# Moving the elementwise helpers of an expert layer from GpSimd to the vector engine, with dense weights split in two steps

## The chip, the cores and the metric

One core of one Trainium2 chip runs the whole kernel. The metric is device time in microseconds (us) of one execution, as the median of several runs. Beside the runs there is one profiled execution with its trace. TensorE is called PE, VectorE DVE, ScalarE ACT, GpSimd POOL, and SP is the engine that only issues transfers.

## The reference

The layer has 1024 latent tokens (and 256 context tokens) of width 1024. A front part (normalisation, an input projection, two groups of recurrent heads, an output projection) gives the stream `x1` and its normalised, modulated form `h2`. The change touches only the second half, an expert layer with 128 x 128 = 16384 experts, each one row `u` and one row `v` of 1024 numbers:

```python
q = (xb @ wq).reshape(PEER_BLOCK, PEER_HEADS, 2, PEER_QDIM // 2)
s = jnp.einsum('tphq,phkq->tphk', q, keys)          # 8 heads x 2 halves x 128 keys
top_s, top_i = lax.top_k(s, PEER_TOPK)              # 16 of each half
cand = top_s[:, :, 0, :, None] + top_s[:, :, 1, None, :]
best_s, best_c = lax.top_k(cand.reshape(...), PEER_TOPK)
idx = i1 * PEER_NKEYS + i2                          # 128 experts a token
g = jax.nn.softmax(best_s, axis=-1)
act = jax.nn.gelu(jnp.einsum('tpkd,td->tpk', u_tab[idx], xb), approximate=False)
return jnp.einsum('tpk,tpkd->td', g * act, v_tab[idx])
```

The result is added to the stream with a gate, and a last RMSNorm follows. All is in fp32.

## The kernel before

The eight blocks of 128 tokens are treated in two ways. **Three blocks (A) are gathered**: for each of the 3 x 128 expert slots, POOL fetches one row of `uv` (u and v side by side, 8 KB) for each of the 128 tokens by an indirect transfer (`fetch`, L996), DVE multiplies the u half with `h2` and sums (L1043), ACT makes gelu and gate (L1008, L1009), and DVE adds the gated v half to an accumulator (L1021). These 384 steps are one generator, `gather`; four row buffers (`uv`) circulate. **Five blocks (B, 640 tokens) are dense**: for all 128 chunks of 128 experts, PE computes U times h2 (L1077, tile `ua`), ACT takes gelu into `w` (L1118), a weight matrix of gates `gch` is multiplied in, and PE multiplies with V (L1465, tile `po`).

PE gets fp32 accuracy from three products of split operands: x = high + low, where ACT makes the high part by a copy (`uh`, `vh`, `wh`, `qhi`) and another engine subtracts it from x to make the low part (`ul`, `vl`, `wl`, `qlo`). One chunk of U needs 48 matmuls of 320 columns; its four quarters of 12 matmuls are what the generator `earlier` yields.

After the front part the stages are, in the order of the program:

- query stage of A (its query weights split with `qlo` on POOL, L1182), then the selection of A's experts (`select`), beside which the first chunks of U and the first gather steps run;
- query stage of B: 16 groups of query matmuls (`pq`), key scores (`sc`) and top-16 searches on DVE, with gather steps and U chunks between;
- selection of B, block by block, again with gather steps and U chunks between;
- building the gate matrices (`gtl`): 80 iterations, each four fp16 operations on DVE (L1354 to L1357: `o`, `oh`, `ol`, `oh`) over 8 tokens, and 16 small matmuls (`gb`) that read them one iteration later;
- a rest of U chunks with nothing else to do on PE; 84 of the 128 chunks (`early`) are computed ahead in all these stages and parked in DRAM (`d_A`);
- the dense stage: 16 groups of 8 chunks, each in two halves of V's columns. In the second half the weights of the next group are made (`produce`, `weights`, `weigh`), and the 44 chunks of U that are left are computed. At the end of each half five sums of `po` go into `accB` on DVE (L1472);
- the last group and the last norm.

Each engine runs its instructions in the order in which the program issues them, so the interleaving is the program's: there is no scheduler. It is steered by two planned clocks, `clock["PE"]` and `clock["DVE"]`. Each step adds its estimated time; `ticks` issues gather steps at given rates; `fill` issues quarters of U chunks as long as PE's clock is less than `lead` = 6 us ahead of DVE's, up to 320 quarters (`spare`).

In the version before, the low part of an early U chunk (`ul`, L1103) is made on POOL when the chunk before it runs, in two halves of 128x512; in B's query stage `qlo` is made on POOL; and while `share[0]` is 2 (B's query stage and selection) every second product of the gather is on POOL too (L1041), and ACT sums it (L1007). The accumulator of the gather lies in two of the eight PSUM banks (`accP`) until the dense stage begins.

## Time and profile before

| | us |
|---|---|
| median of 3 runs | 3157.88 |
| lowest, highest | 3156.48, 3166.47 |
| the profiled execution | 3155.61 |
| span of its trace | 3153.8 |

The trace has 46913 instructions; the mean granted TensorE clock is 0.957 of full speed. Busy times overlap between engines, so they do not add up to the span. A matmul's record covers its whole passage, and matmuls overlap; how fast PE works is read from the distance of their starts.

### The profile page before, as it was taken

How to read it: one execution, taken by the hardware profiler on the slowest of the kernel's cores; microseconds unless marked ns; L12 is line 12 of the kernel's file. 1: busy time of each engine (PE TensorE's matmuls, PEld its weight loads, DVE VectorE, ACT ScalarE, POOL GpSimd, SP SyncE). 2: the span in 40 equal slices, each digit the busy share in tenths (PEclk: the TensorE clock that was granted, in tenths of full speed). 3: DMA queues.
4: the chain of work that ended last, by engine and by line, in shares of the span. 5: the costliest groups of instructions: out<-in, count | busy, mean ns of one | idle time of the engine just before them, and what ended most of it. 6: DMA issues, size and time to landing. Idle time of an engine off the chain costs nothing.

```text
span 3153.8 us, 46913 instructions
## 1 busy us (share of the span) xinstructions
PE 2863.5 (91%) x16937; PEld 2522.2 (80%) x16937; DVE 2508.2 (80%) x4801; ACT 1330.0 (42%) x2915; POOL 997.2 (32%) x768
## 2 busy tenths in 40 slices
PE   7999799998997997878888889999999999999997
PEld 3799677777997987878888888888887788888875
DVE  6633344576798999999999958888888788888885
ACT  4622244564443454455555633333333333333332
POOL 1000113233456776644443432222222222222211
PEclk9999889999998998889999999999999999999998
DMA  6455487645367876768898899999999999999983
GB/s 234 127 187 169 142 258 229 218 144 191 107 245 260 289 275 222 248 234 311 320 318 299 334 367 342 350 339 339 342 344 339 319 331 336 336 338 340 339 301 104
DMA packets 391273, 856.56 MB, mean 272 GB/s; under 512 B 27512, under 2 KB 207352, under 8 KB 341632
## 3 DMA queue, kind: packets, MB, share of 16 engines
q1 hardware_dynamic: 309520, 372.91, 36.9%
q0 software_dynamic: 57600, 411.07, 35.0%
q10 hardware_dynamic: 23920, 69.59, 5.6%
q8 instruction: 133, 2.18, 0.3%
q14 instruction: 100, 0.82, 0.1%
HBM read 746.16 MB, written 107.30 MB: 271 GB/s over the span
## 4 chain that ended last, share of the span: by engine, by line
issue 23%; DVE 18%; PE 7%; POOL 7%; DMA 2%; ACT 1%; POOLq 0%; SPq 0%; DVEq 0%; ACTq 0%
POOL uv L996 7%; PE po L1465 5%; DVE ol L1356 4%; DVE uv L1043 3%; DVE accP L1021 2%; PE ua L1077 2%; DVE oh L1357 2%; DVE oh L1355 2%; DVE o L1354 2%; DMA vr<-uv 1%; DVE acc L1021 1%; DMA uv<-uv,idx 1%; DVE vl L1431 0%; DMA gch<-d_G 0%; ACT wh L1441 0%
## 5 line engine op out<-in xcount | busy, mean ns | idle before, releaser
L996 POOL DMA_INDIRECT uv<-uv,idx x384 | 456.8, 1190 | 1292.1 <-DVE acc L1021 883.6
L1465 PE MATMUL po<-vh,wh 128*128 128x512 f32 x1255 | 499.6, 398 | 50.5 <-DVE accB L1472 44.3
L1077 PE MATMUL ua<-hBhi,uh 128*128 128x320 f32 x2048 | 490.3, 321 | 36.0 <-ACT uh L1102 28.4
L1465 PE MATMUL po<-vl,wh 128*128 128x512 f32 x1255 | 497.8, 397 | 12.0 <-DVE vl L1431 11.9
L1077 PE MATMUL ua<-hBhi,ul 128*128 128x320 f32 x2048 | 479.7, 316 | 22.4 <-POOL ul L1103 22.2
L1465 PE MATMUL po<-vh,wl 128*128 128x512 f32 x1255 | 495.7, 395 | 0.0
L1043 DVE SCALAR_TENSOR_TENSOR uv<-uv,h2a 128x1024 f32<-128x1024 f32 x351 | 441.0, 1256 | 50.7 <-DMA uv<-uv,idx 50.4
L1077 PE MATMUL ua<-hBlo,uh 128*128 128x320 f32 x2048 | 477.9, 315 | 0.0
L1077 PEld LDWEIGHTS ua<-hBhi,uh 128*128 128x128 f32 x2048 | 354.1, 195 | 43.1 <-ACT uh L1102 31.0
L1077 PEld LDWEIGHTS ua<-hBhi,ul 128*128 128x128 f32 x2048 | 351.9, 193 | 27.2 <-POOL ul L1103 27.2
L1077 PEld LDWEIGHTS ua<-hBlo,uh 128*128 128x128 f32 x2048 | 354.7, 194 | 0.0
L1465 PEld LDWEIGHTS po<-vh,wh 128*128 128x128 f32 x1255 | 240.2, 191 | 109.5 <-DVE accB L1472 52.5
L1021 DVE SCALAR_TENSOR_TENSOR acc<-uv,act,acc 128x1024 f32<-128x1024 f32 x237 | 303.3, 1280 | 0.0
L1465 PEld LDWEIGHTS po<-vl,wh 128*128 128x128 f32 x1255 | 240.5, 192 | 64.3 <-DVE vl L1431 16.6
L1465 PEld LDWEIGHTS po<-vh,wl 128*128 128x128 f32 x1255 | 240.1, 191 | 50.9
L1103 POOL TENSOR_TENSOR ul<-ur,uh 128x512 fp32r<-128x512 f32 x170 | 239.3, 1431 | 76.5 <-ACT uh L1102 72.1
L1441 ACT ACTIVATE wh<-w 128x640 fp32r<-128x640 f32 x128 | 94.6, 739 | 396.6 <-DVE w L1438 358.1
L1430 ACT ACTIVATE vh<-vr 128x512 fp32r<-128x512 f32 x251 | 156.4, 625 | 147.7 <-PE po L1465 145.9
L1008 ACT ACTIVATE act<-act 128x1 f32<-128x1 f32 x384 | 75.9, 198 | 335.4 <-DVE uv L1043 333.6
L1021 DVE SCALAR_TENSOR_TENSOR accP<-uv,act,accP 128x1024 f32<-128x1024 f32 x144 | 184.5, 1281 | 13.4 <-ACT act L1009 13.4
L1338 ACT ACTIVATE gtl<-gb 128x512 f32<-128x512 f32 x160 | 160.6, 1113 | 70.1 <-PE gb L1336 58.0
L1442 DVE TENSOR_TENSOR wl<-w,wh 128x640 fp32r<-128x640 f32 x128 | 105.6, 825 | 105.3 <-ACT wh L1441 103.7
(387 smaller groups left out, 5547.1 us busy)
## 6 DMA issues: line engine op xcount, KB each, us to landing
ur<-uC SPq DMA_DIRECT2D x256, 256.0 KB
vr<-uv SPq DMA_DIRECT2D x256, 256.0 KB
d_G<-gtl ACTq DMA_DIRECT2D x80, 512.0 KB
gch<-d_G SPq DMA_DIRECT2D x64, 640.0 KB
d_A<-w ACTq DMA_DIRECT2D x84, 320.0 KB
w<-d_A SPq DMA_DIRECT2D x84, 320.0 KB
wm<-w_mod SPq DMA_DIRECT2D x32, 512.0 KB
qraw<-wq SPq DMA_DIRECT2D x32, 512.0 KB
```

The source lines that it names most:

```text
L996: G.indirect_dma_start(out=t.rearrange("p a d -> p (a d)"), out_offset=None, in_=A["uv"], in_offset=bass.IndirectOffsetOnAxis(ap=idxs[n][: ...
L1008: S.activation(acts[i], acts[i], AF.Gelu)
L1021: V.scalar_tensor_tensor(acc, v, act, acc, op0=ALU.mult, op1=ALU.add)
L1043: V.scalar_tensor_tensor(t, t, 1.0, h2s[n], op0=ALU.mult, op1=ALU.mult, accum_out=acts[i])
L1077: T.matmul(pt[:, :b - a], l[:, kt], m[:, kt, a:b], start=(kt == 0 and wi == 0), stop=(kt == KT - 1 and wi == 2))
L1103: usplit[0].tensor_tensor(ul[:, k], ur, uh[:, k].bitcast(F32), op=ALU.subtract)
L1338: S.activation(gt[:, :, tt:tt + 4].rearrange("p e t -> p t e"), pt.rearrange("p (t e) -> p t e", e=P), AF.Copy, scale=1.0 / 4096.0)
L1356: V.tensor_tensor(ol, oh, pairs(glT, b, t0), op=ALU.mult)
L1430: S.activation(vh, vr[n], AF.Copy)
L1441: S.activation(wh, w, AF.Copy)
L1442: V.tensor_tensor(wl, w, wh.bitcast(F32), op=ALU.subtract)
L1465: T.matmul(po, st[:, b * P:(b + 1) * P], m, start=(start and wi == 0), stop=(stop and wi == 2))
```

## The change

It has six parts. (1) The low part of an early U chunk is made by DVE, as one operation on 128x1024, just as the chunk's first matmuls are issued (`u_low` in `u_side`), and no longer by POOL a chunk ahead; U is loaded in pieces of 128x1024 in three buffers instead of 128x512 in six. (2) In B's query stage `qlo` is made by DVE; A's stays on POOL. (3) The share of the gather's products on POOL is gone: all are on DVE, and ACT's sum of them is gone. So POOL only fetches rows from the selection of A on. (4) The accumulator of the gather lies in SBUF, all eight PSUM banks serve the matmuls, and the copies out of PSUM (`settle`) are gone. (5) The planned DVE clock is charged 2.55 us for a gather step (before 2.35, and 1.75 while every second product was on POOL) and 0.3 us for each quarter of an early chunk. (6) Dense weights are made in two steps: `weights` is a generator that yields between the high part on ACT and the low part on DVE, and `weigh` is called at `b in (1, 3)` of each chunk and between the quarters of a dense U chunk.

```diff
             if i < total:
-                if share[0] and i % share[0] == 0:
-                    prods[i] = t
-                    G.tensor_tensor(t, t, h2s[n], op=ALU.mult)
-                else:
-                    V.scalar_tensor_tensor(t, t, 1.0, h2s[n], op0=ALU.mult, op1=ALU.mult, accum_out=acts[i])
+                V.scalar_tensor_tensor(t, t, 1.0, h2s[n], op0=ALU.mult, op1=ALU.mult, accum_out=acts[i])
...
-    ru = [eru.enter_context(tc.tile_pool(name="ru", bufs=6))]
+    ru = [eru.enter_context(tc.tile_pool(name="ru", bufs=3)), KT]
...
     def u_prep(c):
         if c >= P or isinstance(us[c], tuple):
             return
         uh = up.tile([P, KT, P], F32R, tag="uh", name="uh")
-        ul = up.tile([P, KT, P], F32R, tag="ul", name="ul")
-        for n, ur in enumerate(us[c]):
-            k = slice(4 * n, 4 * n + 4)
+        for k, ur in us[c]:
             S.activation(uh[:, k], ur, AF.Copy)
-            usplit[0].tensor_tensor(ul[:, k], ur, uh[:, k].bitcast(F32), op=ALU.subtract)
-        us[c] = (uh, ul)
+        us[c] = (uh, us[c])
+        if dense[0]:
+            u_low(c)
+
+    def u_low(c):
+
+        uh, parts = us[c]
+        if isinstance(parts, list):
+            ul = up.tile([P, KT, P], F32R, tag="ul", name="ul")
+            for k, ur in parts:
+                V.tensor_tensor(ul[:, k], ur, uh[:, k].bitcast(F32), op=ALU.subtract)
+            us[c] = (uh, ul)
 
     def u_side(c, ahead):
 
         cuts = cuts_of(nd)
+        u_low(c)
         pts = [ubank[0]("ua") for _ in cuts]
...
-            clock["DVE"] += 2.35 - (1.2 / share[0] if share[0] else 0)
+            clock["DVE"] += 2.55
...
             clock["PE"] += next(earlier)
+            clock["DVE"] += 0.3
...
-                    (G if g else V).tensor_tensor(lo, raw, hi.bitcast(F32), op=ALU.subtract)
+
+                    (G if g and ticking >= 0 else V).tensor_tensor(lo, raw, hi.bitcast(F32), op=ALU.subtract)
...
             wh = wp.tile([P, nd], F32R, tag="wh", name="wh")
+            S.activation(wh, w, AF.Copy)
+            yield
             wl = wp.tile([P, nd], F32R, tag="wl", name="wl")
-            S.activation(wh, w, AF.Copy)
             V.tensor_tensor(wl, w, wh.bitcast(F32), op=ALU.subtract)
             ws[c] = (wh, wl)
...
         def weigh():
-            while pend:
-                weights(pend.pop())
+
+            if pend and next(pend[0], True):
+                pend.pop(0)
...
             if c not in first:
                 for d in u_side(plan.index(c), True):
                     ticks(d, share_of)
-            pend.append(c)
+                    weigh()
+            while pend:
+                weigh()
+            pend.append(weights(c))
...
-                        if b == 1:
+                        if b in (1, 3):
                             weigh()
```

How many U chunks and gather steps stand in which stage of the program, counted from the two orders:

| stage | U chunks before | after | gather steps before | after |
|---|---|---|---|---|
| selection of A | 12.75 | 16.25 | 12 | 12 |
| query of B | 1.5 | 6.75 | 35 | 35 |
| selection of B | 23.25 | 33.75 | 31 | 31 |
| gate matrices | 41.5 | 23.25 | 62 | 62 |
| rest, with the first dense chunks | 8 | 7 | 9 | 7 |
| dense | 41 | 41 | 235 | 237 |

On POOL, around B's selection, the order before has, with `r` the index pattern that the selection starts with:

```order
L1041 TENSOR_TENSOR uv<-uv,h2a 128x1024
L1103 TENSOR_TENSOR ul<-ur,uh 128x512 x2
L832 IOTA r_10965 128x256
L996 DMA uv<-uv,idx_6695 128x2048
L1103 TENSOR_TENSOR ul<-ur,uh 128x512 x2
L996 DMA uv<-uv,idx_6695 128x2048
```

and the order after:

```order
L1175 TENSOR_TENSOR qlo<-qraw,qhi 128x1024 x15
L832 IOTA r_7697 128x256
L987 DMA uv<-uv,idx_6695 128x2048 x49
L832 IOTA r_11449 128x256
L987 DMA uv<-uv,idx_6695 128x2048 x31
```

The fetches stand behind no operation on tiles any more; the fifteen `qlo` left are A's.

On PE, in the middle of the gate matrices (about the 35th of the 80 iterations), the order before has a quarter or more of a U chunk after each iteration's products (`o` changes its number with the iteration):

```order
L1336 MATMUL gb<-o_15239,ol 128x128
L1077 MATMUL ua<-hBhi,uh 128x320 x2
L1077 MATMUL ua<-hBlo,uh 128x320 x2
L1077 MATMUL ua<-hBhi,ul 128x320 x2
L1077 MATMUL ua<-hBhi,uh 128x320 x2
```

and the order after goes from one iteration's products straight to the next one's:

```order
L1322 MATMUL gb<-o_16409,ol 128x128
L1321 LDWEIGHTS oh
L1321 MATMUL gb<-o_16490,oh 128x128
L1322 LDWEIGHTS ol
L1322 MATMUL gb<-o_16490,ol 128x128
```

From the 35th iteration to the 80th the order after has no U chunk: the 320 quarters have been issued before.

On DVE, at the end of a second half in the dense stage, the order before has the high and the low step of two weights and then the five sums:

```order
L1431 TENSOR_TENSOR vl<-vr,vh 128x512
L1438 TENSOR_TENSOR w<-w,gch 128x640
L1442 TENSOR_TENSOR wl<-w,wh 128x640
L1043 SCALAR_TENSOR_TENSOR uv,act<-uv,h2a 128x1024
L1021 SCALAR_TENSOR_TENSOR acc<-uv,act,acc 128x1024
L1431 TENSOR_TENSOR vl<-vr,vh 128x512
L1438 TENSOR_TENSOR w<-w,gch 128x640
L1442 TENSOR_TENSOR wl<-w,wh 128x640
L1472 TENSOR_TENSOR accB<-accB,po 128x512 x5
```

and the order after:

```order
L1412 TENSOR_TENSOR vl<-vr,vh 128x512
L1419 TENSOR_TENSOR w<-w,gch 128x640
L1027 SCALAR_TENSOR_TENSOR uv,act<-uv,h2a 128x1024
L1009 SCALAR_TENSOR_TENSOR acc<-uv,act,acc 128x1024
L1424 TENSOR_TENSOR wl<-w,wh 128x640
L1412 TENSOR_TENSOR vl<-vr,vh 128x512
L1419 TENSOR_TENSOR w<-w,gch 128x640
L1424 TENSOR_TENSOR wl<-w,wh 128x640
L1457 TENSOR_TENSOR accB<-accB,po 128x512 x5
```

The first of the two weights now has a gather step between its product and its low part; in the second the two still follow each other on DVE. Of the 128 weights, 29 have a gather step in between, and 99 have nothing.

## Rows read from the trace of the kernel before

**Rows 1.** Stretches: start:end length, busy PE, PEld, DVE, ACT, POOL; PEclk, DMA, GB/s.

```profile
861.00:977.00 116.00, 94.34 (x612) 93.15 (x612) 106.42 (x341) 51.22 (x91) 57.44 (x43) 0.91 0.66 235
977.00:1126.00 149.00, 142.62 (x977) 140.14 (x978) 140.91 (x622) 68.34 (x172) 108.55 (x64) 0.98 0.80 282
1126.00:1358.00 232.00, 182.22 (x1110) 175.84 (x1109) 228.90 (x615) 115.68 (x241) 152.83 (x99) 0.88 0.70 242
1358.00:1820.00 462.00, 401.27 (x3303) 386.93 (x3302) 453.92 (x518) 264.94 (x461) 193.21 (x148) 0.95 0.86 307
1820.00:1888.00 68.00, 61.26 (x395) 60.29 (x396) 34.77 (x45) 24.93 (x58) 27.21 (x20) 0.92 1.00 369
1888.00:3064.00 1176.00, 1124.77 (x5542) 970.11 (x5541) 1019.64 (x1409) 407.62 (x1006) 275.70 (x231) 0.98 0.95 337
3064.00:3154.00 90.00, 67.20 (x275) 52.47 (x274) 52.66 (x103) 22.15 (x52) 13.09 (x10) 0.90 0.33 114
```

**Rows 2.** Timeline of DVE and of POOL near 1405 us: start, length, instruction.

```profile
1405.42 2.50 POOL L1103 TENSOR_TENSOR ul<-ur,uh 128x512 fp32r<-128x512 f32 x2
...
1405.22 3.25 DVE L1356 TENSOR_TENSOR ol<-oh,glT 128x1024 f16<-128x1024 f16 x1
```

**Rows 3.** Groups by line, DVE, 1358 to 1820: count, busy us, mean ns, idle before.

```profile
L1356 DVE TENSOR_TENSOR ol<-oh,glT 128x1024 f16<-128x1024 f16 x80 | 124.5, 1556 | 2.8
...
L1355 DVE TENSOR_TENSOR oh<-io,i2T 128x1024 f16<-128x1024 f16 x80 | 64.5, 806 | 0.0
L1357 DVE TENSOR_TENSOR oh<-oh,ghT 128x1024 f16<-128x1024 f16 x80 | 62.4, 780 | 2.7
L1354 DVE TENSOR_TENSOR o<-io,i1T 128x1024 f16<-128x1024 f16 x80 | 59.1, 738 | 1.7 <-POOL io L1316 1.7
```

**Rows 4.** One line's instructions, L1356: shortest, median, longest in ns.

```profile
L1356 DVE TENSOR_TENSOR ol<-oh,glT x80: 691/692/3328, 1362.0 to 1818.6; 128x1024 f16<-128x1024 f16 x80
```

**Rows 5.** Groups by line and shape, DVE, 861 to 1358.

```profile
L899 DVE TENSOR_TENSOR oh<-oh 128x1024 bf16<-128x1024 bf16 x16 | 30.6, 1909 | 0.5
...
L895 DVE TENSOR_TENSOR oh<-r,rjb 128x2048 bf16<-128x2048 bf16 x8 | 18.3, 2285 | 0.0
...
L895 DVE TENSOR_TENSOR oh<-r,rib 128x2048 bf16<-128x2048 bf16 x8 | 9.7, 1218 | 0.0
```

**Rows 6.** Groups by line, 1888 to 3064: the gather's product on DVE.

```profile
L1043 DVE SCALAR_TENSOR_TENSOR uv<-uv,h2a 128x1024 f32<-128x1024 f32 x234 | 285.1, 1219 | 36.1 <-DMA uv<-uv,idx 35.8
```

**Rows 7.** Operations that move: groups on POOL, 861 to 1888; `qlo` on DVE, whole span.

```profile
L1103 POOL TENSOR_TENSOR ul<-ur,uh 128x512 fp32r<-128x512 f32 x170 | 239.3, 1431 | 76.5 <-ACT uh L1102 72.1 <-issue 3.5
...
L1041 POOL TENSOR_TENSOR uv<-uv,h2a 128x1024 f32<-128x1024 f32 x33 | 81.7, 2474 | 0.6
...
L1182 DVE TENSOR_TENSOR qlo<-qraw,qhi x2: 1215/1220/1226, 772.1 to 977.2; 128x1024 fp32r<-128x1024 f32 x2
```

**Rows 8.** PE's pace: two pieces of the chain; first and last `gb` of an iteration.

```profile
1821.21 27.81 PE ua L1077 x190
...
2363.00 37.03 PE po L1465 x162
...
1402.98 0.23 PE L1335 MATMUL gb<-o,oh 128*128 128x128 f16 x1
...
1403.85 0.22 PE L1336 MATMUL gb<-o,ol 128*128 128x128 f16 x1
```

**Rows 9.** Waits, 1888 or 1890 to 3064: waiter, ended by, us, times, longest.

```profile
DVE wl L1442 <- ACT wh L1441: 97.9, 119, 1.2
...
PE po L1465 <- DVE accB L1472: 42.7, 17, 5.3
```

**Rows 10.** Timeline at the end of a second half: DVE, then PE.

```profile
2435.66 0.83 DVE L1442 TENSOR_TENSOR wl<-w,wh 128x640 fp32r<-128x640 f32 x1 [0.80 <-ACT wh L1441]
2436.40 3.07 DVE L1472 TENSOR_TENSOR accB<-accB,po 128x512 f32<-128x512 f32 x5
...
2437.14 0.80 PE L1465 MATMUL po<-vh,wh 128*128 128x512 f32 x1 [5.31 <-DVE accB L1472]
```

More of the change, by code (lines that the diff above doesn't have):

```diff
@@ L927, in peer @@
     V, S, T, G, Y = nc.vector, nc.scalar, nc.tensor, nc.gpsimd, nc.sync
-    banks, ident, dr, rstd_of = [F["bank"]], F["ident"], F["dr"], F["rstd_of"]
-    bank = lambda name: banks[0](name)
+    bank, ident, dr, rstd_of = F["bank"], F["ident"], F["dr"], F["rstd_of"]
     d_h2, d_x1 = F["d_h2"], F["d_x1"]
@@ L933, in peer @@
     oA, oB = order[:ng], order[ng:]
-    es, esp = ExitStack(), ExitStack()
+    es = ExitStack()
     rows = {}
@@ L973, in peer @@
     gsA = [ga.tile([P, P], F32, name=f"g{n}") for n in range(ng)]
-    accs, psum = {}, []
+    accs = {}
     def row(name):
         return gr.tile([P, D], F32, tag="ha", name=name, bufs=3)
-    def settle(n):
-        t = row("acc")
-        for h in range(2):
-            S.activation(t[:, h * 512:h * 512 + 512], accs[n][:, h * 512:h * 512 + 512], AF.Copy)
-        accs[n] = t
     def gather_all():
         total = ng * P
-        uvs, h2s, acts, prods = {}, {}, {}, {}
+        uvs, h2s, acts = {}, {}, {}
         def fetch(i):
@@ L1014, in add @@
             if k == 0:
-                accs[n] = psum[0] if psum else row("acc")
+                accs[n] = row("acc")
             acc = accs[n]
@@ L1048, in gather_all @@
                 if i % P == 0:
-                    if psum:
-                        settle(i // P - 1)
                     fins.append(finish_steps(oA[i // P - 1], accs[i // P - 1], i == total))
@@ L1080, in project @@
                 yield 2 * 3 * sum(b - a for a, b in cuts) / 2400.0
-    us, wr, ubank, ulim, usplit = {}, {}, [bank], [early + 1], [G]
+    us, wr, ubank, ulim, dense = {}, {}, [bank], [early + 1], [False]
     first = [c for c in range(P) if (c + 1) * early // P != c * early // P]
@@ L1089, in u_load @@
             us[c] = []
-            for k in (0, 4):
-                ur = ru[0].tile([P, 4, P], F32, tag="ru", name="ur")
-                Y.dma_start(ur, A["uC"][plan[c]][:, k:k + 4])
-                us[c].append(ur)
+            m = ru[1]
+            for k in range(0, KT, m):
+                ur = ru[0].tile([P, m, P], F32, tag="ru", name="ur")
+                Y.dma_start(ur, A["uC"][plan[c]][:, k:k + m])
+                us[c].append((slice(k, k + m), ur))
     def u_prep(c):
@@ L1123, in early_all @@
             S.dma_start(d_A[n], wr.pop(c))
-    share = [0]
     gather, earlier = gather_all(), early_all()
@@ L1272, in afterA @@
         gr = es.enter_context(tc.tile_pool(name="gr", bufs=1, side="right"))
-        F["esp"].close()
-        pb = esp.enter_context(tc.tile_pool(name="pb", bufs=6, space=PSUM))
-        pc = esp.enter_context(tc.tile_pool(name="pc", bufs=1, space=PSUM))
-        banks[0] = lambda name: pb.tile([P, 512], F32, tag="b", name=name)
-        psum.append(pc.tile([P, D], F32, name="accP"))
         prime()
@@ L1374, in peer @@
     acc = hB2.tile([P, nb, D], F32, name="accB")
-    ru[0] = es.enter_context(tc.tile_pool(name="ru2", bufs=2))
+    ru[:] = es.enter_context(tc.tile_pool(name="ru2", bufs=2)), KT // 2
     ulim[0] = P
-    usplit[0] = V
-    for n in list(accs):
-        if accs[n] is psum[0]:
-            settle(n)
-    psum.clear()
-    esp.close()
+    dense[0] = True
+    F["esp"].close()
     pa = es.enter_context(tc.tile_pool(name="pa", bufs=8 - len(cuts_of(nd)), space=PSUM))
```

6 lines of the change are left out of this document (removed).

## The prediction

> **What bounds the kernel now.** I first cut the span into stretches and read the busy times of each [rows 1]. The change touches nothing before the selection of A at 861 us and nothing but one helper after 3064, so two parts count: the early stages from 861 to 1888 (1027 us) and the dense stage from 1888 to 3064 (1176 us).
>
> In the early stages DVE is the bound of three of the five stretches: it is busy 106 of 116 us in A's selection, 229 of 232 in B's selection and 454 of 462 in the gate matrices, while PE is busy 94, 182 and 401 [rows 1]. In B's query stage both are full (143 and 141 of 149), and in the rest PE alone works. The longer engine's busy times add to 106 + 143 + 229 + 454 + 61 = 993 us; the stretches take 1027, so 34 us (3.4%) are lost where the two wait for each other.
>
> The second thing to see is that DVE's busy time there is not all work. While POOL subtracts (`ul`, 2.50 us from 1405.42), an fp16 product on DVE that starts at 1405.22 takes 3.25 us and ends with it [rows 2]; the same line's median is 0.69 [rows 4]. The four fp16 lines hold 310.5 us in 320 instructions, which at 0.69 would be 221: 90 us too many [rows 3]. In the selections the 1024-wide sums take 30.6 us for 16, where 0.69 each gives 11, and one line takes 18.3 us with `rjb` and 9.7 with `rib`, the same shape eight times each: another 28 us [rows 5]. Comparing each DVE instruction with the shortest of its line and shape, I get 18, 4, 57 and 99 us in the first four stretches, 178 in all. B's query stage has nearly none, although POOL is busy 109 of its 149 us; its top-16 searches read one tensor.
>
> In the dense stage DVE is busy 1020 us, waits 98 us for ACT before the low part of a weight [rows 9] and 36 us for fetched rows [rows 6]: 1154 of 1176. So DVE's chain fills this stage, though PE is busy 1125. PE waits 42.7 us in 17 places for the sums of `po` [rows 9]; in one of them it stands for 5.31 us, while DVE waits 0.80 for ACT, makes `wl` and only then sums [rows 10].
>
> **Part by part: POOL is emptied.** If only operations on tiles hold DVE up, all 178 us go. That the fetches don't is seen in the dense stage: POOL fetches for 276 us there [rows 1], and the gather's product has a mean of 1219 ns [rows 6]. That row is of one kind of DVE operation; the fp16 ones are never seen beside fetches alone for long, so the gain lies between 178 us and what remains if a fetch holds DVE like a subtraction, which is a rival below. I take 178.
>
> The Trainium skill (GPSIMD Engine Reference, section Key points) says that GpSimd shares its SBUF interfaces with VectorE and contends with DVE instructions that have two SBUF inputs. The trace agrees for the subtractions (0.69 to 3.25 us); read as a rule for the fetches too, it would leave about 58 us, which the 1219 ns speak against.
>
> **What DVE gets instead.** 85 low parts of U, 15 `qlo` and 33 products, each some 1.2 us: `qlo` on DVE took 1.22, the product 1.22 [rows 7, 6], less a few hundredths since the next starts before an operation's end. That is 133 x 1.2 = 160 us. DVE's sum falls by 18 us, and 2 of the 149 early gather steps move to the dense stage (2 x 2.4 us).
>
> **Where the U chunks go.** A chunk is 48 matmuls at 27.81/190 = 0.146 us [rows 8], 7.0 us of PE. With the dearer planned DVE clock PE's chunks are issued earlier: 57 stand ahead of the gate matrices where 38 did, and the last 46 of the 80 iterations have none (the table and order above). So I add each stretch anew, PE beside DVE, and the longer one counts:
> - A's selection: PE 16.25 x 7.03 = 114; DVE 106 - 18 + 16 x 1.2 = 107. Longer: 114.
> - B's query: PE 143 - 1.5 x 7 + 6.75 x 7.03 = 180; DVE 141 - 4 + (15 + 18 + 7) x 1.2 = 185. Longer: 185.
> - B's selection: PE 33.75 x 7.03 = 237 and about 5 for 27 other matmuls; DVE 229 - 57 + (15 + 34) x 1.2 = 231. Longer: 242.
> - Gate matrices: one iteration without POOL's delays is (454 - 99)/80 = 4.44 us of DVE; an iteration's 16 small matmuls take about 0.93 us (0.87 from first to last start [rows 8]). The first 34: PE 23.25 x 7.03 + 34 x 0.93 = 195; DVE 34 x 4.44 + 23 x 1.2 = 179. The other 46: DVE 204, PE 43. Longer: 399.
> - Rest: 68 - 7 = 61.
>
> The sum is 114 + 185 + 242 + 399 + 61 = 1001 us, 8 more than the 993 of before: what DVE gains in the gate matrices (454 to 399) is lost again, since PE becomes the bound ahead of them and stands nearly empty in their second half. How much the engines lose to each other can't be read from the trace of before. It is bounded by the 34 us of now, if the lockstep is no worse; by 15, if emptying POOL and PSUM takes most of it away; and by 7% (75 us), since DVE now makes `ul` at the very place where PE needs it. I take 36, near the value seen: 1037, so +10 us (from -11 to +49).
>
> **Weights in two steps.** One wait for ACT costs 97.9/119 = 0.82 us [rows 9]. The idea would remove all of it, but the order shows that 99 of the 128 low parts still follow their product directly on DVE, so that DVE waits for ACT as before; 29 have a gather step in between. That saves 29 x 0.82 = 24 us of a chain that fills the stage; two more gather steps cost 5. I take -17 for the dense stage (1159), between 0, if the time comes back as waiting for fetched rows, and -43, if all of PE's waits for the sums go. PE's own pace is no obstacle: 3570 matmuls at 37.03/162 = 0.229 and 1972 at 0.146 make 1105 us [rows 8, 1].
>
> **Edits costed at nothing.** U in pieces of 512 KB instead of 256: the same bytes in the same buffer space, and the issue stands at the same place of the queue; it is hidden by the two chunks (14 us) between load and use. If that cover went, PE would wait for `uh`. The accumulator in SBUF: one DVE operation as before. ACT loses 33 sums and the copies out of PSUM; ACT is busy about half of the time [rows 1].
>
> The sum: 3155.6 + 10 - 17 = 3149 against the profiled execution; the median of the runs stands 2.3 us higher, which is inside the error, and I say **3150**.
>
> **Rivals.**
> 1. *The low part of U on the path (slower).* In the stages before the 35th iteration DVE has 702 us of work against PE's 736, and each of some 79 chunks can begin only when DVE, in its own order, has made `ul`. DVE's pieces are uneven: a step of the selection and one or two gather steps make 5 to 7 us in a row. For it: DVE was busy 97 to 99% there when it was the bound. Against it: the program issues PE's work 6 us ahead of DVE's, and `uh` is ready a chunk earlier. At 0.5 us a chunk beyond my 36 us it costs 40: 3190. It decides the sign from about 0.2 us a chunk (16 us: 3166).
> 2. *Both losses go (faster).* With POOL no longer in the chain and eight PSUM banks the early loss is 15 us, and the freed 24 us on DVE let it catch up before each second half ends, so that PE's waits vanish: 3155.6 - 11 - 43 = 3102. For it: 24 us over 15 such ends are 1.6 us each, against 42.7/15 = 2.8. Against it: DVE stays the fuller chain.
> 3. *Fetches hold DVE as well, so that emptying POOL does less than it says.* POOL was busy 539 us in the early stages [rows 1]; 147 fetches of 1.2 us are a third of that, so a third of 178, 58 us, would stay: 3207. The 1219 ns speak against it.
>
> **How the numbers follow.** My forecast has 0.42, with a range of its own of 3136 to 3164; rival 1 has 0.26, rival 2 has 0.24, rival 3 has 0.05, and 0.03 is left for a load that comes late. The range has to reach most of rivals 1 and 2: 3105 to 3190. A measurement of this kernel can tell about 0.3%, 9.5 us, from no change. Faster than 3148: 0.18 of the forecast's chance and nearly all of rival 2, 0.41. Within: 0.20 of the forecast's and 0.06 of the rivals' mild ends, 0.26. Slower: 0.33.
>
> **What would show it.** Right: the fp16 lines near 0.69 us in the mean; POOL busy with fetches alone after A's query stage; B's query stage near 190 us and B's selection near 250; the gate matrices near 415, with PE idle in their second half; `wl` waiting for ACT some 75 us instead of 98; PE's waits for the sums near 25. Wrong: fp16 lines still well above 0.69 (rival 3); PE waiting for DVE's `ul` for more than 50 us (rival 1); a B query stage no longer than 160 us, which would say that the issued order doesn't set PE's bound.

## The result and the profile after

The changed kernel takes 3408 us in the median beside 3161 us of the kernel before in the same runs: a ratio of 1.078, with a 95% interval of 1.075 to 1.080. The prediction was 3150 us with a range from 3105 to 3190. Where did 250 us come from? The same stretches as in [rows 1], read from the changed kernel (from, to and length in us; busy us of PE, its weight loads, DVE, ACT and POOL with instructions; granted clock; DMA share; GB/s):

```profile
869.00:1014.00 145.00, 123.51 (x781) 121.30 (x782) 107.80 (x355) 56.85 (x89) 23.18 (x16) 0.93 0.62 218
1014.00:1255.00 241.00, 192.88 (x1251) 191.03 (x1251) 186.58 (x704) 62.09 (x161) 40.34 (x32) 0.88 0.55 192
1255.00:1562.00 307.00, 253.62 (x1613) 249.62 (x1612) 231.74 (x668) 111.87 (x212) 58.15 (x37) 0.92 0.61 214
1562.00:2085.00 523.00, 321.05 (x2426) 299.52 (x2425) 380.40 (x531) 224.81 (x358) 79.58 (x62) 0.73 0.65 239
2085.00:2150.00 65.00, 55.53 (x336) 53.85 (x336) 35.70 (x46) 20.47 (x47) 13.74 (x9) 0.91 0.93 352
2150.00:3322.00 1172.00, 1126.34 (x5548) 970.86 (x5547) 1023.78 (x1412) 407.70 (x1009) 274.61 (x232) 0.98 0.95 339
```

The dense stage is 1172 us beside 1176. The loss lies in the five early stages: 1281 us beside 1027. DVE is busy 942 us there and PE 947, so **no engine is full any more**. In B's query stage both engines are busy 187 to 193 of 241 us, in B's selection 232 and 254 of 307, in the gate matrices 380 and 321 of 523. DVE's busy times there are within 3 us of the forecast; the time went into waiting, and some of it into a slower PE (granted clock 0.73 in the gate matrices, 0.95 before). The waits of these stages (engine and line that waited, releaser: us, times, longest):

```profile
ACT w L1110 <- PE ua L1059: 251.2, 59, 13.3
ACT gtl L1324 <- PE gb L1322: 217.8, 51, 13.7
...
PE ua L1059 <- DVE ul L1094: 203.2, 52, 10.6
DVE o L1340 <- PE gb L1322: 138.8, 29, 9.8
...
DVE acc L1009 <- ACT act L997: 64.2, 25, 6.2
DVE v L840 <- ACT s L1203: 35.8, 6, 7.6
```

PE waits for DVE's `ul`, and DVE waits for PE's products `gb`, or through ACT for what PE delivers. One turn of it stands in the timeline of DVE in the gate matrices (start, duration, instruction, and in brackets the idle time before it and what ended it):

```profile
1805.13 0.69 DVE L1343 TENSOR_TENSOR oh<-oh,ghT 128x1024 f16<-128x1024 f16 x1
1805.74 1.22 DVE L1027 SCALAR_TENSOR_TENSOR uv<-uv,h2a 128x1024 f32<-128x1024 f32 x1
...
1806.88 1.28 DVE L1009 SCALAR_TENSOR_TENSOR acc<-uv,act,acc 128x1024 f32<-128x1024 f32 x1
1808.08 1.22 DVE L1094 TENSOR_TENSOR ul<-ur,uh 128x1024 fp32r<-128x1024 f32 x1
1817.03 0.69 DVE L1340 TENSOR_TENSOR o<-io,i1T 128x1024 f16<-128x1024 f16 x1 [7.73 <-PE gb L1322]
```

and in that of PE:

```profile
1803.22 0.45 PE L1059 MATMUL ua<-hBlo,uh 128*128 128x320 f32 x2
1809.35 0.90 PE L1059 MATMUL ua<-hBhi,ul 128*128 128x320 f32 x2 [5.68 <-DVE ul L1094]
1810.05 0.74 PE L1059 MATMUL ua<-hBhi,uh 128*128 128x320 f32 x2
...
1815.30 0.46 PE L1059 MATMUL ua<-hBlo,uh 128*128 128x320 f32 x2
1815.60 0.46 PE L1059 MATMUL ua<-hBhi,ul 128*128 128x320 f32 x2
1815.89 0.23 PE L1321 MATMUL gb<-o,oh 128*128 128x128 f16 x1
...
1816.77 0.22 PE L1322 MATMUL gb<-o,ol 128*128 128x128 f16 x1
```

PE has started a chunk with the two products that need only the high part and stands 5.68 us at the third, which needs `ul`; that subtraction stands on DVE behind a whole iteration with a gather step. When it comes, PE does the rest of three quarters of the chunk and only then the sixteen small products of the iteration before, because they are queued behind these quarters. DVE's next `o` overwrites a buffer that these products read, so DVE stands 7.73 us. The engines **take turns**: DVE, chunk, products, DVE. A pair of matmuls soon behind the wait takes 0.74 us where one takes 0.46 later: PE's clock had fallen to the lower of its two levels (granted 0.50 from 1809.3 to 1812 us, 1.00 again from 1814).

That DVE and PE do what they are given in the order of their queues is what the Trainium skill says too (PSUM — Partial Sum Buffer, section Engine vs sequencer instructions): the queues of ScalarE, VectorE and GpSimd are strict FIFO, and matmuls start and complete in program order. The two timelines agree: from 1809.35 to 1815.89 us the products stand 6.5 us behind chunk matmuls that they don't need.

Two parts of the prediction's picture came true. The fp16 line that held 124.5 us in [rows 3] is at its clean 0.69 us, and no DVE instruction of the early stages is longer than the short ones of its kind by more than 0.15 us, so all 178 us of hold-ups are gone:

```profile
L1342 DVE TENSOR_TENSOR ol<-oh,glT 128x1024 f16<-128x1024 f16 x80 | 55.3, 692 | 2.8
```

And in the dense stage DVE's wait for the high part of a weight is where it was forecast, beside 97.9 us in [rows 9], though the stage gained next to nothing by it:

```profile
DVE wl L1424 <- ACT wh L1421: 74.5, 91, 0.9
...
PE po L1450 <- DVE accB L1457: 36.8, 19, 4.4
...
DVE vl L1412 <- ACT vh L1411: 26.7, 30, 3.5
```

### The profile page after: what moved, and what is told of

It reads as the page before. It is cut to its first block, busy times and chain, and to the rows that moved or that the text cites. A ratio compares the mean times of both kernels' runs of the same rounds, so it can differ in the third digit from the quotient of the medians.

```text
span 3408.3 us, 46434 instructions
## 1 busy us (share of the span) xinstructions
PE 2930.2 (86%) x16937; PEld 2581.5 (76%) x16937; DVE 2491.0 (73%) x4967; ACT 1280.5 (38%) x2760; POOL 671.5 (20%) x550
## 4 chain that ended last, share of the span: by engine, by line
issue 39%; POOL 10%; PE 8%; DVE 4%; ACT 1%; DMA 1%; POOLq 0%; ACTq 0%; SPq 0%; DVEq 0%
POOL uv L987 10%; PE ua L1059 5%; PE po L1450 3%; DVE acc L1009 1%; DVE ul L1094 1%; DMA uv<-uv,idx 0%; DVE uv L1027 0%; DMA vr<-uv 0%; DMA out<-ft 0%; DVE accB L1457 0%; DVE vl L1412 0%; ACT ex L858 0%; ACT uh L1083 0%; ACT w L1110 0%; POOLq L987 0%
## 5 line engine op out<-in xcount | busy, mean ns | idle before, releaser
L987 POOL DMA_INDIRECT uv<-uv,idx x384 | 487.2, 1269 | 1914.2 <-DVE acc L1009 1658.0
L1059 PE MATMUL ua<-hBhi,ul 128*128 128x320 f32 x2048 | 499.8, 327 | 203.2 <-DVE ul L1094 203.2
L1009 DVE SCALAR_TENSOR_TENSOR acc<-uv,act,acc 128x1024 f32<-128x1024 f32 x381 | 487.8, 1280 | 70.0 <-ACT act L997 67.0
L1059 PEld LDWEIGHTS ua<-hBhi,ul 128*128 128x128 f32 x2048 | 363.8, 201 | 217.4 <-DVE ul L1094 217.0
L1027 DVE SCALAR_TENSOR_TENSOR uv<-uv,h2a 128x1024 f32<-128x1024 f32 x384 | 467.2, 1217 | 39.6 <-DMA uv<-uv,idx 39.1
L1059 PEld LDWEIGHTS ua<-hBhi,uh 128*128 128x128 f32 x2048 | 364.3, 199 | 14.7 <-ACT w L1110 9.5
L1110 ACT ACTIVATE w<-ua 128x320 f32<-128x320 f32 x256 | 97.6, 433 | 358.2 <-PE ua L1059 346.4
L1321 PE MATMUL gb<-o,oh 128*128 128x128 f16 x640 | 116.5, 269 | 119.4 <-DVE oh L1343 116.2
L1412 DVE TENSOR_TENSOR vl<-vr,vh 128x512 fp32r<-128x512 f32 x251 | 171.4, 686 | 29.4 <-ACT vh L1411 28.5
L1094 DVE TENSOR_TENSOR ul<-ur,uh 128x1024 fp32r<-128x1024 f32 (+1 forms) x171 | 158.4, 949 | 38.4 <-ACT uh L1083 38.4
```

The lines of the kernel that those rows point to most:

```text
L987: G.indirect_dma_start(out=t.rearrange("p a d -> p (a d)"), out_offset=None, in_=A["uv"], in_offset=bass.IndirectOffsetOnAxis(ap=idxs[n][: ...
L1009: V.scalar_tensor_tensor(acc, v, act, acc, op0=ALU.mult, op1=ALU.add)
L1027: V.scalar_tensor_tensor(t, t, 1.0, h2s[n], op0=ALU.mult, op1=ALU.mult, accum_out=acts[i])
L1059: T.matmul(pt[:, :b - a], l[:, kt], m[:, kt, a:b], start=(kt == 0 and wi == 0), stop=(kt == KT - 1 and wi == 2))
L1094: V.tensor_tensor(ul[:, k], ur, uh[:, k].bitcast(F32), op=ALU.subtract)
L1110: S.activation(w[:, a:b], pt[:, :b - a], AF.Gelu)
```

## Experiments

The table gives the length of the stages in us of each profiled execution, from event to event: the first chunk matmul, B's first query matmul, B's last key score, the first `o`, the last `gb`, the first gated weight. (Cut so, before has 1012 us where the round windows of [rows 1] gave 1027, and the changed kernel 1260.) In brackets the first 34 iterations of the gate matrices. The last column is the median of the runs (of the kernel before, the medians of its sets beside the others), and for the kernels with four runs or more the ratio to the kernel before with its 95% interval.

| kernel | A sel. | B query | B sel. | gate matrices (34) | rest | early sum | program |
|---|---|---|---|---|---|---|---|
| before | 116 | 152 | 232 | 460 (191) | 53 | 1012 | 3152 to 3161 |
| changed | 145 | 241 | 296 | 533 (314) | 45 | 1260 | 3408, 1.078 [1.075, 1.080] |
| x1 changed, `ul` a chunk ahead | 133 | 186 | 257 | 411 (192) | 44 | 1030 | 3179, 1.0058 [1.004, 1.0077] |
| x2 changed, `ul` not read | 124 | 186 | 239 | 410 (191) | 45 | 1004 | 3151, 0.998 [0.996, 0.999] |
| x3 changed, old charges | 127 | 231 | 251 | 619 (277) | 45 | 1274 | 3422 |
| x5 changed, ahead and old charges | 123 | 182 | 233 | 408 (172) | 44 | 990 | 3136, 0.992 [0.989, 0.995] |
| x6 before, `ul` on DVE ahead | 120 | 154 | 230 | 424 (173) | 52 | 979 | 3125, 0.989 [0.986, 0.992] |
| x15 before, `ul` on DVE at the chunk | 122 | 174 | 236 | 609 (256) | 53 | 1196 | 3350 |
| x7 changed, products first | 143 | 241 | 296 | 466 (243) | 44 | 1189 | 3343 |
| x8 changed, `ul` on POOL | 135 | 222 | 293 | 443 (226) | 44 | 1137 | 3280 |
| x11 changed, late gelu | 133 | 242 | 289 | 533 (314) | 44 | 1240 | 3389 |
| x12 x11 and products first | 134 | 243 | 289 | 472 (250) | 43 | 1181 | 3328 |
| x13 x11 and a third `uh` | 132 | 243 | 279 | 533 (314) | 45 | 1231 | 3381 |
| x14 x13 and products first | 131 | 242 | 279 | 466 (244) | 44 | 1162 | 3314 |
| x4 before, two-step weights | 115 | 152 | 232 | 460 (191) | 54 | 1012 | 3148, 0.997 [0.995, 0.998] |
| x9 x6 and two-step weights | 119 | 154 | 229 | 421 (173) | 49 | 974 | 3118, 0.986 [0.984, 0.988] |
| x10 x6 and `vl` in between | 120 | 153 | 229 | 420 (173) | 51 | 974 | 3091, 0.979 [0.976, 0.981] |

### Place, amount or plan: x1, x2, x3

Three theories stood for the lost time: turn-taking by the place of `ul` (R), too much work for DVE (Q), and the dearer charges that move PE's chunks forward (C). **x1** makes the low part one chunk earlier:

```diff
-    us, wr, ubank, ulim, dense = {}, {}, [bank], [early + 1], [False]
+    us, wr, ubank, ulim, dense = {}, {}, [bank], [early + 1], [True]
```

> The changed kernel, but DVE's subtraction for a chunk of U stands one chunk earlier, behind the first matmuls of the chunk before, as in the dense stage. Nothing else: the same operations on the same engines, the same order of PE's matmuls. Theory R (turn-taking): in the changed kernel the chunk's low part is queued on DVE where PE wants it, PE's later products that DVE waits for stand behind that chunk, so that the two engines work in turn. Then the early stages fall from 1281 us to 1040-1090, PE's waits for the low part of U from 203 us to under 40, the program to 3150-3210. Theory Q (DVE simply has too much to do, wherever it stands): the early stages stay near 1281 and the program at 3380-3410. Theory C (the dearer planned DVE clock lets PE's chunks be queued too early, ahead of what DVE waits for): PE's order is as it was, so the program stays above 3330.

**x2** leaves everything at its place and takes PE's wait away:

```diff
-        for n, d in enumerate(project(pts, None, us[c][0], us[c][1], bhi, blo, cuts)):
+        for n, d in enumerate(project(pts, None, us[c][0], us[c][int(dense[0])], bhi, blo, cuts)):
```

> The changed kernel with DVE's subtraction at its place, but the third product of an early chunk reads the high part a second time and not the low part: the low part of U is left out of the early chunks' results. The same number of matmuls of the same size on PE and the same operations on DVE in the same order; only PE's wait for DVE at the start of a chunk is gone. Theory R: as much as moving it ahead, 3150-3210, early stages 1040-1090. Theory Q: 3380-3410, since DVE does what it did. Theory C: above 3330, since the orders are what they were.

**x3** takes back the planned clock:

```diff
-            clock["DVE"] += 2.55
+            clock["DVE"] += 2.35
...
-            clock["DVE"] += 0.3
+            clock["DVE"] += 0.0
```

> The changed kernel with the planned DVE time of before: 2.35 us for a gather step and nothing for a piece of a chunk, so that PE's chunks are queued later (more of them in the gate matrices). Theory R: every early chunk still waits for a subtraction that stands at its place on DVE, so the early stages stay above 1200 us and the program above 3330. Theory C: the early stages come back to 1040-1100 and the program to 3160-3230.

Measured: 3179, 3151 and 3422 us. R holds, Q and C fall. With the same work on the same engines, 229 of the 247 us go when `ul` is made a chunk earlier, and 257, more than the whole loss, when PE doesn't wait for it. The plan alone moves the loss about (more in the gate matrices, less in B's selection) and leaves it as large. Compare the windows of the first 34 iterations, with the same matmuls in them, first of the changed kernel, then of x1:

```profile
1551.00:1865.00 314.00, 225.65 (x1614) 215.97 (x1613) 177.92 (x238) 112.31 (x183) 41.40 (x28) 0.87 0.51 190
```

```profile
1447.00:1639.00 192.00, 192.00 (x1617) 188.43 (x1616) 177.65 (x238) 113.44 (x183) 37.24 (x27) 1.00 0.86 311
1639.00:1858.00 219.00, 95.83 (x820) 83.94 (x819) 210.30 (x305) 113.52 (x177) 40.90 (x36) 0.53 0.85 305
```

In the changed kernel PE and DVE are busy 226 + 178 = 404 us in 314, so they overlap in some 90 at the least. In x1 PE is busy all of 192 us, and DVE's 178 lie inside. PE's 226 us for what takes 192 are the clock: 0.87 beside 1.00. x1's second row is the other 46 iterations: there PE has little to do, its clock is at 0.53, and DVE sets the time.

### Place and plan together; the kernel before with one part: x5, x6, x15

**x5** has the edits of x1 and x3.

> The changed kernel with both edits: the subtraction a chunk ahead, and the planned DVE time of before, by which PE's chunks are spread further into the gate matrices. Theory R with the sums of the longer engine: once the turn-taking is gone the place of the chunks counts, since DVE (942 us) and PE (947) have about the same work there; evenly mixed, the early stages fall from the 1030 us of the subtraction ahead alone to 980-1015, the program to 3125-3165. If the place of the chunks doesn't matter: 3170-3190.

**x6** is the kernel before with the subtractions on DVE a chunk ahead, and nothing else:

```diff
-    us, wr, ubank, ulim, usplit = {}, {}, [bank], [early + 1], [G]
+    us, wr, ubank, ulim, usplit = {}, {}, [bank], [early + 1], [V]
```

> The kernel before with the low parts of U on DVE, at the place that they had in the program (a chunk ahead), and nothing else moved: POOL keeps its products and query subtractions, PE its order. DVE gets 170 x 0.65 = 110 us and loses the part of the 178 us of hold-ups that POOL's 170 subtractions cause (by their share of POOL's tile time, 239 of 360 us, some 120). Theory R (nothing wrong with the engine, only with the place): early stages within 20 us of the 1012 of before, the program 3140-3180. Theory Q (too much work for DVE): above 3220.

**x15** is x6 with the subtraction moved to the changed kernel's place:

```diff
             S.activation(uh[:, k], ur, AF.Copy)
-            usplit[0].tensor_tensor(ul[:, k], ur, uh[:, k].bitcast(F32), op=ALU.subtract)
-        us[c] = (uh, ul)
+        us[c] = (uh, us[c])
...
         cuts = cuts_of(nd)
+        u_low(c)
         pts = [ubank[0]("ua") for _ in cuts]
```

> The kernel before with the low part of U on DVE at the changed kernel's place (as the chunk is queued) and nothing else of the change: it stands beside the run with the same operations on DVE a chunk ahead (3124.8 us, early stages 979). Theory R: the place alone makes the loss, early stages 1180-1300 us, program 3320-3450. If it takes the other parts of the change as well (the dearer clock, one accumulator in SBUF, query parts on DVE): 3140-3250.

The three measured 3136, 3125 and 3350 us. x5 and x15 lie in the ranges of theory R; x6 is faster than its range (3140 to 3180), as POOL's hold-ups of DVE fell by some 140 us, by the comparison with the shortest of each kind, where I had taken 120. Theory Q's 3220 is far off. x6 and x15 differ in the place alone, and that place costs 217 us (979 to 1196); so it needs no other part of the change. With the place mended, the charges do count: 1030 us with the dear ones, 990 with the old. And x6, with the one part of the change that empties POOL of its 170 subtractions, is faster than the kernel before by 1.1% and no slower than x5 (0.992), which has the other parts as well.

x6 shows one thing more. These are the waits of x6 and of x15 in the early stages:

```profile
PE ua L1077 <- DVE ul L1103: 56.1, 24, 6.7
```

```profile
PE ua L1077 <- DVE ul L1112: 260.3, 70, 10.8
DVE o L1364 <- PE gb L1346: 186.7, 49, 7.6
```

PE waits 56 us for `ul` in x6 too, in a kernel that is faster than before. What costs is the second row of x15: in x6 DVE has no wait for `gb`. One engine's wait is slack; two that release each other are a ring.

### Where the ring closes: x7, x11, x12, x13, x14

**x7** queues the products of the iteration before ahead of the chunk:

```diff
-                    dve(2.4, rhog)
-                    g_store()
                     if late:
                         products(*late)
+                    dve(2.4, rhog)
+                    g_store()
```

> The changed kernel with one edit in the gate matrices: PE's sixteen products of the iteration before are queued ahead of this iteration's chunk and not behind it. Theory R says that there the ring closes through them: DVE's next indicator needs the buffer that these products read, they stand behind a chunk, the chunk waits for a low part that stands behind DVE's iteration. So the first 34 iterations fall from 314 us to 195-230, the other stages stay (145, 241, 296), and the program falls to 3290-3330. If the ring isn't closed there (PE's waits for the low part are all that counts), the 314 us stay: 3390-3410.

It gave 3343 us: the first 34 iterations fell from 314 to 243, the gate matrices as a whole from 533 to 466, the other stages stayed to 2 us. The direction and the stage are as expected; 243 is above the 195 to 230 that I gave, and the program above its 3330. DVE's wait for `gb` has fallen from 139 to 5 us, but its accumulation now waits for ACT's gate operations (x7, early stages):

```profile
DVE acc L1009 <- ACT act L997: 129.6, 52, 6.7
...
DVE o L1340 <- PE gb L1322: 4.9, 2, 3.3
```

So a second way round was open, through ACT. I took it to be the gelu `w` of a chunk that PE hasn't done, behind which the gather's gate operations stand on ACT; for the gate matrices this was wrong, as x14 shows below. **x11** queues that gelu most of a chunk later:

```diff
+            if n == 3 and not dense[0]:
+                gelu()
...
-        w = wr[plan[c]] = up.tile([P, nd], F32, tag="we", name="w", bufs=3)
-        for pt, (a, b) in zip(pts, cuts):
-            S.activation(w[:, a:b], pt[:, :b - a], AF.Gelu)
+        held.append((plan[c], pts))
```

> The changed kernel with one edit in the early stages: ACT's gelu of a chunk's sums is queued most of a chunk later, so that the small gate operations of the gather, for which DVE's accumulation waits, don't stand behind a chunk that PE hasn't done. Theory R says that in the selections, where DVE needs nothing of PE, the turn-taking closes through ACT's queue alone: B's selection falls from 296 us to 245-265, A's from 145 to 125-140; B's query stage (scores behind the chunk in PE's own queue) and the gate matrices (products behind the chunk) stay within 10 us of 241 and 314+219. Program 3345-3380. If ACT's queue isn't what closes it, 296 stays and the program is at 3395-3410.

**x12** has both edits.

> The changed kernel with the late gelu and with PE's products ahead of the chunk (which alone brought the first 34 iterations from 314 to 243 us and the program to 3343). The low part of U stays at its place on DVE. Theory R: the first 34 iterations lose the rest of the turn-taking too, 195-215 us, beside B's selection at 245-265: program 3260-3310, and PE may go on waiting for the low part without harm. If the wait itself is what costs, wherever the ring is closed: 3330-3345.

Both missed: B's selection 289 us, the program 3389; and 3328 for x12 with 250 us for the 34 iterations. The waits of x11 say why:

```profile
ACT uh L1083 <- PE ua L1059: 227.2, 56, 13.7
```

ACT no longer stands before `w` (251 us in the changed kernel) but before the next chunk's `uh`, whose buffer PE still reads. The edit had not freed ACT. **x13** adds a third buffer for `uh` and pays for it with loads of U two chunks ahead instead of three; **x14** adds x7's edit.

```diff
-    ru = [eru.enter_context(tc.tile_pool(name="ru", bufs=3)), KT]
+    ru = [eru.enter_context(tc.tile_pool(name="ru", bufs=2)), KT]
...
-        uh = up.tile([P, KT, P], F32R, tag="uh", name="uh")
+        uh = (ru[0] if c % 3 == 2 and not dense[0] and c < early else up).tile([P, KT, P], F32R, tag="uh", name="uh", bufs=1 if c % 3 == 2 and not dense[0] and c < early else 2)
...
-                u_load(c + (3 if c + 1 < early else 2))
+                u_load(c + 2)
```

> The changed kernel with the late gelu and, so that ACT doesn't stand before the next chunk's high part instead (227 us for a buffer that PE still reads), a third buffer for the high parts; the loads of U run two chunks ahead and not three, to make room. The low part stays at its place on DVE. If ACT's queue closes the ring in the selections, the wait of DVE's accumulation for the gate operations (26.7 us in B's selection of the changed kernel) goes below 8 and B's selection falls from 290-296 to 255-272 us; if PE's queue does (transposes behind chunks), the 30 us of waiting for the transposed gates stay, and B's selection with them: 275-290. B's query stage and the gate matrices as in the changed kernel. Program 3350-3390.

> The same with PE's products ahead of the chunk in the gate matrices. What is left there with the products ahead alone (243 us for the first 34 iterations, 58 us of it in waits of DVE's accumulation for ACT's gate operations) should be ACT's queue: then 195-215 us, and that wait below 15; program 3260-3310. If it is PE's wait for the low part itself: 235-250 and 3320-3345.

x13 brings B's selection to 279 us. Its waits of DVE in that stage are

```profile
DVE ghT L1307 <- ACT gt L1306: 29.8, 4, 9.4
DVE acc L1009 <- ACT act L997: 11.1, 4, 3.9
```

beside 30.5 and 26.7 us in the changed kernel. The wait for the gate operations shrank, the one for `ghT` stayed: it comes from PE's transposes, which stand behind a chunk in PE's own queue (x1, with the same transposes there, waits 4.0 us). I had said that DVE needs nothing of PE in the selections; it needs these four. So in B's selection the ring closes on both ways. Freeing ACT was worth 17 us there (296 to 279). PE's way still holds 30 us of waiting in x13, and x1, where that wait is 4.0, has a stage 22 us shorter; no run opened PE's way alone.

In both kernels ACT had found a third thing to wait for, the load of U (142 us in x13, 135 in x14), for which the edit left a buffer less. But in the 34 iterations it waits 4 us or less for loads. There x14 stayed at 244 us, as x7 was at 243. That lies in the 235 to 250 that I gave for the case that PE's wait for the low part itself costs; the waits of these 34 iterations of x14 say otherwise:

```profile
ACT gtl L1337 <- PE gb L1335: 110.9, 28, 9.6
DVE acc L1009 <- ACT act L997: 59.8, 25, 6.6
...
PE ua L1059 <- DVE ul L1094: 33.4, 20, 4.5
```

DVE is idle for 67 of the 244 us, and 60 of them end with a gate operation of ACT. One of these waits, on ACT and on DVE:

```profile
1574.19 1.99 ACT L1337 ACTIVATE gtl<-gb 128x512 f32<-128x512 f32 x2 [9.58 <-PE gb L1335]
```

```profile
1576.56 1.28 DVE L1009 SCALAR_TENSOR_TENSOR acc<-uv,act,acc 128x1024 f32<-128x1024 f32 x1 [6.64 <-ACT act L997]
```

ACT copies the products `gb` out into `gtl`, and the edit queues that copy, too, ahead of the gather's gate operations. The products stand on PE behind the quarters that the iteration before has queued, these wait for `ul`, and `ul` stands on DVE behind the accumulation. So what is left of the ring in the gate matrices closes through `gtl`, not through the gelu: in x7, too, ACT stood 97 us before `gtl` in these iterations and 14 before `w`. This is read from the waits; **no run took that wait away**.

**x8** leaves the place and changes the engine:

```diff
-                V.tensor_tensor(ul[:, k], ur, uh[:, k].bitcast(F32), op=ALU.subtract)
+                (V if dense[0] else G).tensor_tensor(ul[:, k], ur, uh[:, k].bitcast(F32), op=ALU.subtract)
```

> The changed kernel with the subtraction of an early chunk at its new place in the program but on POOL, so that it stands behind fetches and not behind DVE's work. If the place alone matters (whichever engine makes it, it comes as the chunk is queued), the early stages stay above 1200 us and the program above 3340. If it is that it stands in DVE's own queue behind the work for which PE has yet to deliver, the turn-taking ends, and POOL's hold-ups of DVE come back in part (170 of the 178 us at most): early stages 1030-1130, program 3170-3280.

The program took 3280 us, the early stages 1137, 7 above what I gave. DVE's wait for `gb` is 23 us (139 in the changed kernel), PE still waits 107 us for the low part, and by the comparison with the shortest of each kind DVE is held up by 125 us again:

```profile
L1342 DVE TENSOR_TENSOR ol<-oh,glT 128x1024 f16<-128x1024 f16 x80 | 94.7, 1184 | 2.8
```

That makes 1.18 us in the mean again beside 0.69. So in the gate matrices the ring has nearly opened off DVE's queue even at the late place: the first 34 iterations take 226 us, with DVE busy 200, beside 192 in x1. In B's selection it has not (293 us beside 296, and 257 in x1), with DVE busy 230. POOL's subtractions stand there in part behind fetches that wait 48 us for DVE's accumulation, and DVE still waits 34 us for `ghT` and 25 for ACT's gate operations. The 107 us that x8 is slower than x1 in the early stages are therefore not the hold-ups alone; how they divide isn't shown.

### The dense stage: x4, x9, x10

**x4** is the kernel before with the weights in two steps, as in the change's diff.

> The kernel before with the weights of the dense stage in two steps and nothing else. The prediction's term: 29 of 128 low parts no longer wait for ACT, worth 24 us less at most and 17 taken: 3137-3150 beside 3161, DVE's wait for the weights' high part down from 98 us to about 75. Rival: the saved wait comes back as another (rows fetched, or the low part of V waiting for ACT), as in the changed kernel's dense stage, which lost only 4 us: 3153-3161.

It is faster by 0.3% (5 to 15 us). DVE's wait for `wh` fell from 98.7 us in 120 places to

```profile
DVE wl L1443 <- ACT wh L1440: 83.4, 102, 0.9
```

and the stage by 6 us, from the first gated weight to the last `po` (1268 to 1262; this cut takes in the last group). **x9** adds it to x6.

> The kernel before with two edits: the low parts of U on DVE a chunk ahead (alone 3124.8 us, ratio 0.989) and the weights in two steps (alone 0.997). If the two gains lie in different stages and add: 0.9857 of before, about 3115. If the dense stage's gain comes from POOL or from what DVE's order of before gives, it doesn't add: 3122-3128.

3118 us, a ratio of 0.986: the gains add (0.989 x 0.997 = 0.986), though the interval reaches to 0.988, where the rival's 3122 begins. **x10** takes x6 and puts an operation that doesn't need ACT between product and low part: V's low part.

```diff
                 S.activation(vh, vr[n], AF.Copy)
+                if pend:
+                    next(pend[0])
                 V.tensor_tensor(vl, vr.pop(n), vh.bitcast(F32), op=ALU.subtract)
...
             S.activation(wh, w, AF.Copy)
+            yield
+            wl = wp.tile([P, nd], F32R, tag="wl", name="wl")
             V.tensor_tensor(wl, w, wh.bitcast(F32), op=ALU.subtract)
...
-                        if b == 1:
+                        if b == 0:
                             weigh()
```

> The kernel before with the low parts of U on DVE a chunk ahead, and in the dense stage another order of the same operations: a chunk's product with its gates goes ahead of the low part of V, and the low part of the weights behind it, so that 122 of 128 low parts of a weight have a 0.69 us operation between them and their product (in the two-step version 24). The prediction's idea taken as far as it goes: DVE's wait for the weights' high part falls from 98 us to 10-35, and since DVE's chain fills the stage, the dense stage from 1176 us to 1105 (PE's own pace) to 1140: program 3055-3100. Rival (the wait comes back, as PE's wait for the sums or as DVE's wait for fetched rows or for V's high part): 3105-3125.

3091 us, **2.1% faster than the kernel before** (1.9 to 2.4%) and the fastest of all. The stage is 1238 us by the cut of x4, beside 1268. Its waits:

```profile
DVE wl L1445 <- ACT wh L1442: 24.4, 108, 0.8
...
PE po L1470 <- DVE accB L1477: 24.2, 17, 5.9
```

Of the 98 us on DVE 74 went; the stage got 30 shorter. Cut as in [rows 1], from the first `po` to the last chunk matmul, it takes 1147 us beside 1176, 7 above the 1105 to 1140 that I gave, and PE is now the fuller engine, busy 1117 of 1147 us:

```profile
1852.00:2999.00 1147.00, 1117.25 (x5541) 963.06 (x5540) 1021.57 (x1407) 415.08 (x1007) 276.47 (x231) 0.99 0.96 345
```

## Why the prediction was wrong

**The step that failed is one term: the loss of 36 us between the engines, with its bound of 75.** The sums of the longer engine were good to some 10 us a stage. Without the ring, x2 shows them: 124, 186, 239 and 410 us, where the prediction had 114, 185, 242 and 399. The last stage, cut as in [rows 1] at the first `po`, is 66 us in x2 beside 61. Together that is 1025 beside 1001, so that a loss of 24 us is left, near the 36. The changed kernel, by the same cut, has 1281 - 1001 = 280 us of loss, nearly four times the upper bound.

**Why the bound was no bound.** I took it as a share of the stage (7%), as if the low part's place made only the grain coarser. What the place did was to close a ring, and in a ring much of the two engines' times adds where before the larger counted: in the first 34 iterations 404 us of busy time took 314, where x1 took 192. That should have been asked of the queues, not of the busy times: when `ul` stands at DVE's present place, what that DVE needs next stands behind the chunk that needs `ul`? In the gate matrices the answer was in the code, in `products`, which is queued behind the chunks.

**Rival 1 named the mechanism and priced it wrongly.** It gave 0.5 us a chunk beyond the 36, 3190 us; measured against x1 it is 230 us over some 80 chunks, 2.9 us each. (Its 736 us of PE count DVE's 185 in B's query stage; with PE's 180 it is 731, which changes nothing.) Its counterargument, that PE's work is issued 6 us ahead of DVE's, fell: that lead is made of the very chunks that wait, and the products stand behind them. Its mark, PE waiting for `ul` for more than 50 us, was not a good one either: x6 waits 56 and is faster than before. The mark in these runs is both engines waiting for each other.

**POOL emptied: right.** All 178 us of hold-ups went, and fetches hold nothing up, as [rows 6] had suggested; rival 3 falls. x8 brings 125 us of it back with the subtractions alone. The Trainium skill's sentence (GPSIMD Engine Reference, section Key points) that GpSimd contends with DVE instructions that have two SBUF inputs agrees for tile operations: 0.69 us become 1.18 in the mean. For the fetches these runs show none of it.

**Work given to DVE: right.** In the first 34 iterations DVE is busy 178 us where 179 were forecast, in the other 46 it is 210 beside 204. The gate matrices' second half came as forecast too, 219 us with PE busy 97 of them and the granted clock at 0.54, which costs nothing there, since DVE is busy 210.

**Chunks moved forward: right in direction, not in price.** I had the shift at 8 us in the sum. x1 against x5 measures the dear charges at 40 us once the ring is open (1030 against 990): with them PE is the longer engine ahead of the gate matrices and idle behind.

**Weights in two steps: 17 us taken, 0 to 43 given.** This term was too large, too. Alone the edit brought 5 to 15 us, 6 in the stage (x4); in the changed kernel 4 by the cut of [rows 1] and nothing by that of x4 (1268 us as before). DVE's wait for `wh` shrank by the 24 us forecast in the changed kernel, but its wait for `vh` rose from 17 to 27 and PE's waits for the sums came down to 37, not 25. That 99 low parts still follow their product directly was read rightly from the order; x10 shows what the idea is worth when they don't.

**The edits at nothing** (loads of 512 KB, the accumulator in SBUF): ACT's wait for a loaded piece of U is 11 us in the changed kernel's early stages beside 9 before, and an accumulation takes 1.28 us in SBUF as it does in PSUM (x15, which keeps the PSUM row).

## What to carry to other kernels

Before a helper is moved to its consumer's moment, write down for each engine's queue what stands behind the consumer and whether the helper's engine needs it next: if it does, the two engines take turns, and much of their times adds, whatever their shares of busy time are. A third engine's queue can close the same ring (by x14's waits, ACT's with `gtl`). The same operation on the same engine one step earlier made 229 us of difference here (x1 beside the changed kernel), and 217 in the early stages (x6 beside x15). A wait for another engine's result shrinks when an independent operation of the same queue is put between (98 to 24 us in x10), and a two-step helper helps only where such an operation really stands there.

## What the runs showed of the hardware

- Indirect fetches on POOL leave DVE alone here, fp16 operations too: beside fetches only (POOL busy 80 of 523 us), `ol` keeps 0.692 us in the mean of 80, while tile operations on POOL stretch it to 1.18 (x8).
- The clock is part of a ring's price. In the first 34 iterations the granted clock was 0.87 in the changed kernel and 1.00 in x1, and the same matmuls kept PE busy 226 us and 192. Behind an idle time of 5.68 us the granted clock was 0.50 and a pair of matmuls took 0.74 us, later 1.00 and 0.46; these are the two levels, 1.2 and 2.4 GHz.
- A freed in-order queue finds its next wait: ACT stood 251 us before `w` in the changed kernel, 227 us before `uh` in x11, and 142 us for the load of U in x13, while the early stages changed by 2%.
